# Where 576 token columns are divided between two matmuls, in four feed forwards

## The chip, the cores and the metric

The kernel runs on one core of one Trainium2 chip, in one launch. The metric is device time in microseconds. The engines are called PE (TensorE, matmuls), PEld (TensorE's weight loads, which overlap its matmuls), DVE (VectorE), ACT (ScalarE), POOL (GpSimd) and SP (SyncE, which issues most DMAs).

## What is computed

A step of a trunk of two layers of width 1024, for 512 prompt tokens and 8 sequences of 8 sample tokens, 576 tokens together. Each layer is a half feed forward, a mixer and another half feed forward, each behind an RMS norm that is shifted, scaled and gated by rows that are computed from a condition (adaLN). The mixer of layer 0 is a gated linear attention beside a spatial gate, that of layer 1 an mLSTM. What matters here is the feed forward, of hidden width 2816:

```python
def _swiglu(x, w_gate, w_up, w_down):
    return (jax.nn.silu(x @ w_gate) * (x @ w_up)) @ w_down

h = _modulate(_rms_norm(x, W['ffn_norm'][l, 0]), sh1, sc1)
x = x + 0.5 * g1[:, None, :] * _swiglu(h, W['ffn_w_gate'][l, 0], W['ffn_w_up'][l, 0], W['ffn_w_down'][l, 0])
```

It is computed four times: (layer 0, first), (0, second), (1, first), (1, second), called (0,0), (0,1), (1,0), (1,1) below.

## The kernel before, in words

Activations lie with features on the 128 partitions and tokens along the free axis: `x` is 8 tiles of 128 x 576. The first 512 columns are the prompt's, the last 64 the sample's. A product takes a 128 x 128 block of weights as the stationary operand and streams the tokens past it.

Precision is kept by splitting. A weight `w` and an activation `x` in float32 are each cut into a high and a low part of type float32r (`wh`, `wl`, `xh`, `xl`), and a product is `wh xh + wh xl + wl xh`. `w_split` (L183 on ACT, L184 on DVE) cuts the weights, which arrive by DMA in the order of use; `hilo` (L402, L403) cuts the activations.

`tile3` issues the three terms for one block of weights. A matmul writes at most 512 columns, a bank of PSUM, so the 576 token columns are divided: each term is two matmuls of 288 columns (`HT`) with the same weights, L203. `dense_gen` runs `tile3` over the row tiles of a product and hands the accumulator, `psd`, to whoever evacuates it; there are two such accumulators of two banks each. Before, each half of `psd` starts at the beginning of its bank, and readers see the two halves as a 3-D view (`v2`).

In `ffn` the hidden features come in three groups of 8, 7 and 7 tiles. For each tile the gate and the up product run over 8 row tiles; ACT takes the silu of the first (L470), DVE multiplies with the second (L477), and the result is cut into `hh` and `hl`. After a group the 8 output tiles run over the group's tiles (`psd<-hh` and `psd<-hl` in the profile), and `x_add` (L411, L413, L415) adds them to `x` on DVE, the prompt's columns with one gate and the sample's with one gate per sequence. So a feed forward has 22 x 2 x 8 row tiles for gate and up and 8 x 22 for down, three terms each. In layer 0 and before, `fill` puts matmuls of the adaLN rows (L256) between the products.

At the end of a feed forward `finish` sums the last squares over the features (`sumsq`, L319, L325), and the next `norm` follows from their sum. The mixers use the same `dense`, `pair_gen` and `x_add`; other matmuls are issued by their own lines, in float32 or float32r: L537 (float32r, 512 columns), L781 and L782 (float32r, 384 columns), L1399 and L256 (float32, 512 columns), L1498 and L1500 (one and four columns; the latter in float32r). A matmul in float32 stands in the profile as two rows.

The order on each engine is the order in which the program issues the instructions.

Of the kernel before, what the change touches and what calls it, by code (L numbers as in the profile page):

```python
# [25 lines left out]
PB = TP - HT  # L26
# [9 lines left out]
def _lhs(w):  # L36
    """[K, M] -> [128, (K/128) M]: row k*128+p, column m sits at [p, k*M+m]."""
    k, m = w.shape
    return w.reshape(k // P, P, m).transpose(1, 0, 2).reshape(P, -1)
# [22 lines left out]
def rows_units(key, c0):  # L62
    """Four units of two row tiles each, of 512 columns, for products that keep tokens on partitions."""
    for u in range(4):
        yield (1024, lambda a, u=u: _lhs(a[key][0][u * 256:(u + 1) * 256, c0:c0 + 512]))


def pair_units(key, m0, order):
    """Two column tiles of a square weight in turns of four row tiles."""
    for h in range(0, len(order), 4):  # L70
        yield (KD * P, lambda a, h=h: np.concatenate([_lhs(a[key][0][k * P:k * P + P, m * P:m * P + P]) for m in (m0, m0 + 1) for k in order[h:h + 4]], 1))
# [37 lines left out]
# parts of the constants that sit side by side, [128, ...] each  # L109
# [5 lines left out]
def cut(t, parts):  # L115
    """Views of a tile that holds such parts."""
    out, c0 = {}, 0
    for name, shape in parts.items():
        n = int(np.prod(shape))
        v = t[:, c0:c0 + n]  # L120
        if len(shape) > 1:
            ax = "abcd"[:len(shape)]
            v = v.rearrange(f"p ({' '.join(ax)}) -> p {' '.join(ax)}", **dict(zip(ax, shape)))
        out[name] = v
        c0 += n
    return out


class Trunk:
    def __init__(self, ctx, tc, ins, outs):  # L130
# [19 lines left out]
        # weight stream  # L150
# [7 lines left out]
        # ada stream  # L158
# [5 lines left out]
        self.queue = []  # L164

# [32 lines left out]
    def tile3(self, ps, wh, wl, xh, xl, start, stop):  # L198
        """ps[:, half, :HT] (+)= w^T x over one 128-row tile, w = wh + wl and x = xh + xl."""
        mm = self.nc.tensor.matmul  # L200
        for j, (w, xx) in enumerate(((wh, xh), (wh, xl), (wl, xh))):
            for a in range(2):
                mm(ps[:w.shape[1], a, :HT], w, xx[:, a * HT:(a + 1) * HT], start=start and j == 0, stop=stop and j == 2)  # L203

    def dense_gen(self, xs, order, evac):
        ps = self.psd.tile([P, 2, 512], F32, name="psd", tag="psd")
        n = len(order)
        for j in range(n):
            if j % 4 == 0:
                wh, wl = self.piece()  # L210
            c = slice(j % 4 * P, j % 4 * P + P)
            k = order[j]
            self.tile3(ps, wh[:, c], wl[:, c], xs[0][k], xs[1][k], j == 0, j == n - 1)
            if j < n - 1:
                yield
        evac(ps)
        yield
# [7 lines left out]
    def pair_gen(self, xs, order):  # L225
        """Two products whose weights come in turns of four row tiles."""
        ps = [self.psd.tile([P, 2, 512], F32, name="psd", tag="psd") for _ in range(2)]
        for j in range(len(order)):
            if j % 4 == 0:
                ws = [self.piece(), self.piece()]  # L230
            c = slice(j % 4 * P, j % 4 * P + P)
            for (wh, wl), p in zip(ws, ps):
                self.tile3(p, wh[:, c], wl[:, c], xs[0][order[j]], xs[1][order[j]], j == 0, j == len(order) - 1)
            yield ps if j + 1 == len(order) else []
# [41 lines left out]
    def mod_post(self, blk, m):  # L276
        """Keeps a shift, a norm's gain with its scale, or a gate (halved before the half sub-layers)."""
        nc = self.nc
        l, w = (2, blk - 18) if blk >= 18 else divmod(blk, 9)
        s = l * 3 + w // 3  # L280
        if w % 3 == 0:
            nc.vector.tensor_copy(self.sh[:, s], m)
        elif w % 3 == 1:
            nc.vector.scalar_tensor_tensor(out=self.am[:, s], in0=m, scalar=1.0,
                                           in1=self.gn[:, s, :].unsqueeze(2).to_broadcast([P, KD, NC]), op0=ALU.add, op1=ALU.mult)
        else:
            nc.vector.tensor_scalar(out=self.gm[:, s], in0=m, scalar1=1.0 if w == 5 else 0.5, scalar2=None, op0=ALU.mult)
# [7 lines left out]
    def fill_mm(self, n):  # L295
        """Up to n steps, none that evacuates a group."""
# [12 lines left out]
    def rsqrt(self, out, in_, scale, tmp):  # L309
        """out = (in_ * scale + EPS) ** -0.5"""  # L310
# [22 lines left out]
    def norm(self, s, ss, hook=None, mid=None):  # L333
        """xh + xl = rms_norm(x) * am + shift."""
# [45 lines left out]
    def final(self, s, ss):  # L380
        """The last norm, into the output."""
# [23 lines left out]
    def x_add(self, m, ps, g):  # L405
        """x[:, m] += g * ps, g by sequence."""
        nc = self.nc
        x = self.x[:, m, :]
        for a, n in ((0, HT), (1, PB)):
            xa = x[:, a * HT:a * HT + n]  # L410
            nc.vector.scalar_tensor_tensor(out=xa, in0=ps[:, a, :n], scalar=g[:, m, 0:1], in1=xa, op0=ALU.mult, op1=ALU.add)  # L411
        t = self.work.tile([P, TS], F32, name="xs", tag="xs")
        nc.vector.tensor_tensor(out=t.rearrange("p (b t) -> p b t", b=NS), in0=ps[:, 1, PB:HT].rearrange("p (b t) -> p b t", b=NS),  # L413
# [4 lines left out]
    def ada_pool(self, ctx, name, bufs, stop):  # L418
        """Room for adaLN weights that are loaded ahead, for the units before `stop`."""
# [4 lines left out]
    def first_norm(self, ss):  # L424
        """The norm that waits for its adaLN rows."""
# [13 lines left out]
    def ffn(self, l, i, ss, fills, gap):  # L439
# [7 lines left out]
        with ExitStack() as ctx:  # L447
# [6 lines left out]
            xs = self.xk()  # L454
            f0 = 0
            v2 = lambda t: t.rearrange("p (a n) -> p a n", a=2)
            for gi, n in enumerate(FGROUPS):
                hh = [hp.tile([P, T], F32R, name=f"hh{j}", tag=f"hh{j}") for j in range(n)]
                hl = [hp.tile([P, T], F32R, name=f"hl{j}", tag=f"hl{j}") for j in range(n)]
                for j in range(n):  # L460
# [9 lines left out]
                    nc.scalar.activation(v2(sg), pg[:, :, :HT], AF.Silu)  # L470
# [6 lines left out]
                    nc.vector.tensor_tensor(out=v2(h), in0=v2(sg), in1=pu[:, :, :HT], op=ALU.mult)  # L477
# [16 lines left out]
                f0 += n  # L494
            self.finish(ss)
# [5 lines left out]
    def finish(self, ss):  # L501
        """The last squares; adaLN matmuls fill TensorE until the next norm is through."""
# [25 lines left out]
    def rows_gen(self, evac):  # L528
        """x @ w for 512 columns with tokens on partitions."""
# [14 lines left out]
    def mixer0(self, ss):  # L544
        nc = self.nc
        tt, act = nc.vector.tensor_tensor, nc.scalar.activation
        v2 = lambda t: t.rearrange("p (a n) -> p a n", a=2)
        xs = self.xk()
        done = set()
        with ExitStack() as ctx:  # L550
# [13 lines left out]
            def ev_q(b, w):  # L564
                def evac(ps):
                    act(v2(qk[:, b, w]), ps[:, :, :HT], AF.Copy, scale=1.0 if w else 0.125)
# [14 lines left out]
            def ev_u(g):  # L581
                def evac(ps):
                    tt(out=v2(z[:, g]), in0=v2(z[:, g]), in1=ps[:, :, :HT], op=ALU.mult)
# [46 lines left out]
    def gla_gates(self, w2, ss, z, lh, ll, vr, vrs, sg):  # L630
        """The norm, the rows of log decays, and the spatial gate before its u."""
# [32 lines left out]
        for h in range(4):  # L664
            ps = self.dense(self.xk(), KS)
            act(sg[:, h].rearrange("p (a n) -> p a n", a=2), ps[:, :, :HT], AF.Silu)
# [57 lines left out]
    def gla_post(self, o, sg, gln, heads):  # L724
        """Norm over each head's values, gain and gate."""
# [34 lines left out]
    def gla(self, c, w2, lh, ll, vr, vrs, masks, bmask, qk, v, o, qm, ready, half):  # L760
# [10 lines left out]
        def expo(i, b):  # L771
            """exp of the summed log decays: from each block's middle, from the start and to the end of the rows."""
# [23 lines left out]
        def scores(i, b, hh, ke, qe):  # L796
            """S[s, t], level by level of the blocks that part s from t."""
# [124 lines left out]
    def operands(self, ctx, name):  # L922
        """Room for the parts of the normed rows."""
# [55 lines left out]
    def ml_in(self, w1):  # L979
        """The input projection, the convolution, and the rows that the gates give."""  # L980
# [4 lines left out]
        v2 = lambda t: t.rearrange("p (a n) -> p a n", a=2)  # L985
# [25 lines left out]
        def xm_block(f, ps):  # L1011
            xm = w1.tile([P, T], F32, name="xm", tag="xm", bufs=4)
            xms[f] = xm
            act(v2(xm), ps[:, :, :HT], AF.Copy)
# [46 lines left out]
        for f in range(MB):  # L1061
# [4 lines left out]
            act(v2(zs), ps[:, :, :HT], AF.Silu)  # L1066
# [14 lines left out]
    def ml_rows(self, w, pg):  # L1081
        """Per token and head: a = log input gate - F, F the summed log forget gates, M the running maximum of a, m = F + M."""
# [3 lines left out]
        v2 = lambda t: t.rearrange("p (a n) -> p a n", a=2)  # L1086
# [158 lines left out]
    def ml_sample(self, h):  # L1245
        """The sample's queries, keys and values, its scores and denominators."""
# [61 lines left out]
    def stack(self, h, j):  # L1308
        """Three copies of the sample's rows, for keys with their weights."""
# [6 lines left out]
    def ml_den(self, pd, em):  # L1316
        """max(den ** 2, exp(-m) ** 2)"""
# [7 lines left out]
    def ml_head(self, h):  # L1325
# [6 lines left out]
        # the prompt's projections  # L1332
        i4 = lambda t: t.rearrange("p (i c) -> p i c", c=P)

        def keys(j):
            """Keys with tokens on partitions, and their weights."""
# [28 lines left out]
        # its scores  # L1365
# [22 lines left out]
        # denominators and numerators  # L1388
# [23 lines left out]
    def ml_norm(self, pn, d2):  # L1412
        """The rows over their denominators, normed: (pn - mean) * (var + EPS * d2) ** -0.5."""
# [13 lines left out]
    def z_load(self, h, t):  # L1427
        """The gate with its gain and with skip and input, for a tile of tokens."""
# [4 lines left out]
    def ml_post(self, hn, t, z):  # L1433
        """Back to features on partitions, with gain, skip and gate, in two parts."""
# [18 lines left out]
    def ml_units(self, h, den):  # L1453
        """The sample's matrices: what they add to the outputs, and their update."""
# [29 lines left out]
    def ml_state(self, h):  # L1484
        """The prompt's matrix, and both groups' normalisers."""
# [44 lines left out]
def levels(n, chunk, sizes):  # L1530
    """0/1 patterns (the first over 16) of which rows s the decays of row t sum over, and of the pairs that a level holds."""
# [51 lines left out]
def pack(a):  # L1583
    """The inputs as the program takes them: cut, transposed and put side by side."""
# [72 lines left out]
```

## Time and profile before

| what | value |
|---|---|
| median of 2 runs | 2811.63 us (2810.9 to 2812.36) |
| span of the profiled execution, first to last instruction | 2806.7 us |
| TensorE busy | 2731.7 us, 97%, 19182 matmuls |
| VectorE busy | 1281.7 us, 46% |
| ScalarE busy | 839.5 us, 30% |
| mean granted TensorE clock | 0.983 |
| feed forward (0,0), from its first to its last product | 36.7 to 480.7 us |
| (0,1) | 822.1 to 1267.6 us |
| (1,0) | 1278.6 to 1704.6 us |
| (1,1) | 2363.5 to 2789.3 us |

The profiled execution is known by its span; the times of the runs lie some 5 us above it, which is what lies around the first and the last instruction. The busy time of a group of instructions is the time in which at least one of them is under way. The length of a single matmul's row (some 296 ns) holds its way through the array, in which the next one has already started; what a matmul costs in a stream is the time from its start to the next one's start, read from rows of the timeline.

### The profile page before, as it was taken

The page shows a single profiled execution, that of the slowest core. Times are in us where ns is not written, and L with a number is a line of the kernel's source. Part 1 is how long each engine was busy: PE and PEld are TensorE (multiplying, and loading weights), DVE is VectorE, ACT ScalarE, POOL GpSimd, SP SyncE. Part 2 cuts the span into 40 slices and gives each one's busy share as a digit, 9 for nine tenths or more (in the row PEclk, how much of TensorE's full clock was granted, in tenths as well). Part 3 has the DMA queues.
Part 4 walks back from the last instruction along what each step waited for, and adds up shares of the span by engine and source line. Part 5 has one row for each costly group of instructions (what it writes and reads, how often), then busy time and mean ns, then how long its engine had stood idle before and what let it go on. Part 6 is the DMA issues. An engine that isn't in the chain of part 4 may idle for free.

```text
span 2806.7 us, 45768 instructions
## 1 busy us (share of the span) xinstructions
PE 2731.7 (97%) x19182; PEld 2462.0 (88%) x19182; DVE 1281.7 (46%) x2578; ACT 839.5 (30%) x1508; POOL 193.4 (7%) x263
## 2 busy tenths in 40 slices
PE   6999999999999999999999999999999999999997
PEld 4899998787788999998999997998567667999997
DVE  4233334346562333345333337654776676333334
ACT  4222223432242222234222234334323324222223
POOL 1000000022110000001000004300110111000000
PEclk8999999999799999999999999999999999999999
DMA  7533224221146332223222244467885665222222
GB/s 288 214 122 136 83 82 138 67 77 45 56 166 255 136 136 83 84 83 113 83 83 77 85 143 164 151 177 240 304 295 213 235 244 195 89 83 82 84 76 73
DMA packets 114741, 388.49 MB, mean 138 GB/s; under 512 B 19416, under 2 KB 37096, under 8 KB 95720
## 3 DMA queue, kind: packets, MB, share of 16 engines
q1 hardware_dynamic: 102088, 336.62, 35.0%
q0 software_dynamic: 4880, 35.06, 3.2%
q10 hardware_dynamic: 7568, 13.90, 1.3%
q8 instruction: 151, 2.47, 0.3%
q14 instruction: 54, 0.44, 0.0%
HBM read 324.95 MB, written 60.59 MB: 137 GB/s over the span
## 4 chain that ended last, share of the span: by engine, by line
PE 90%; DVE 4%; ACT 2%; issue 1%; DMA 1%; POOL 1%; DVEq 0%; SPq 0%; ACTq 0%; POOLq 0%
PE psd L203 74%; PE psc L1494 2%; PE psd L537 2%; PE psa L256 1%; PE psc L1382 1%; PE psa L1465 1%; PE psc L1399 1%; PE psc L805 1%; DVE yn L363 1%; DMA adaw<-ada 1%; POOL qe L788 1%; DVE xl L353 1%; PE psd L1473 1%; PE psc L1348 1%; PE psd L1351 0%
## 5 line engine op out<-in xcount | busy, mean ns | idle before, releaser
L203 PE MATMUL psd<-xh,whi 128*128 128x288 f32 x3648 | 794.7, 299 | 11.5 <-ACT xh L364 7.7
L203 PE MATMUL psd<-xl,whi 128*128 128x288 f32 x3648 | 786.8, 297 | 7.2 <-DVE xl L353 6.8
L203 PE MATMUL psd<-xh,wlo 128*128 128x288 f32 x3648 | 784.3, 297 | 1.5 <-DVE wlo L184 1.5
L184 DVE TENSOR_TENSOR wlo<-wraw,whi 128x512 fp32r<-128x512 f32 (+1 forms) x696 | 459.2, 698 | 454.0 <-ACT whi L183 449.6
L203 PEld LDWEIGHTS psd<-xh,whi 128*128 128x128 f32 x3648 | 589.5, 190 | 55.1 <-issue 18.0
L203 PEld LDWEIGHTS psd<-xl,whi 128*128 128x128 f32 x3648 | 590.2, 190 | 12.5 <-DVE xl L353 11.9
L203 PEld LDWEIGHTS psd<-xh,wlo 128*128 128x128 f32 x3648 | 590.9, 190 | 1.8 <-DVE wlo L184 1.8
L183 ACT CAST whi<-wraw 128x512 fp32r<-128x512 f32 (+1 forms) x696 | 400.4, 609 | 411.0 <-PE psd L203 371.5
L203 PE MATMUL psd<-hh,whi 128*128 128x288 f32 x1408 | 301.4, 296 | 0.0
L203 PE MATMUL psd<-hh,wlo 128*128 128x288 f32 x1408 | 301.3, 295 | 0.0
L203 PE MATMUL psd<-hl,whi 128*128 128x288 f32 x1408 | 300.9, 295 | 0.0
L411 DVE SCALAR_TENSOR_TENSOR x<-psd,gm,x 128x288 f32<-128x288 f32 (+1 forms) x272 | 119.2, 480 | 345.3 <-PE psd L203 345.3
L203 PEld LDWEIGHTS psd<-hh,whi 128*128 128x128 f32 x1408 | 226.7, 188 | 1.7 <-issue 1.7
L203 PEld LDWEIGHTS psd<-hl,whi 128*128 128x128 f32 x1408 | 226.6, 188 | 0.0
L203 PEld LDWEIGHTS psd<-hh,wlo 128*128 128x128 f32 x1408 | 226.4, 188 | 0.0
L477 DVE TENSOR_TENSOR h<-sg,psd 128x576 f32<-128x576 f32 x88 | 66.4, 754 | 349.2 <-PE psd L203 349.2
L402 ACT CAST hh<-h 128x576 fp32r<-128x576 f32 x88 | 59.3, 674 | 488.7 <-DVE h L477 488.7
L470 ACT ACTIVATE sg<-psd 128x576 f32<-128x576 f32 x88 | 57.4, 653 | 359.8 <-PE psd L203 359.8
L349 POOL TENSOR_TENSOR yn<-x,rstd 128x576 f32<-128x576 f32 x30 | 49.3, 1651 | 1067.3 <-ACT rstd L377 1010.1
L403 DVE TENSOR_TENSOR hl<-h,hh 128x576 fp32r<-128x576 f32 x88 | 66.8, 759 | 65.2 <-ACT hh L402 65.2
L203 PE MATMUL psd<-hz,whi 128*128 128x288 f32 x512 | 95.5, 309 | 0.9 <-DVE kc L1286 0.9
L1477 DVE SCALAR_TENSOR_TENSOR cu<-cu,wd,psd 128x512 f32<-128x512 f32 x128 | 87.0, 742 | 15.2 <-PE psd L1473 14.5
(331 smaller groups left out, 2251.6 us busy)
## 6 DMA issues: line engine op xcount, KB each, us to landing
wraw<-wall SPq DMA_DIRECT2D x284, 512.0 KB, 3.6
adaw<-ada SPq DMA_DIRECT2D x80, 1024.0 KB, 7.5
cu<-mC SPq DMA_DIRECT2D x32, 1024.0 KB, 5.7
Cs<-cu POOLq DMA_DIRECT2D x32, 1024.0 KB, 6.1
wraw<-wall SPq DMA_DIRECT2D x64, 448.0 KB, 3.2
szp<-zp SPq DMA_DIRECT2D x32, 256.0 KB, 2.6
bx<-sx SPq DMA_DIRECT2D x16, 512.0 KB, 6.0
zt<-szp SPq DMA_DIRECT2D x16, 512.0 KB, 7.7
```

What stands on the lines that cost most here:

```text
L183: nc.scalar.copy(hi[:, :n], raw)
L184: nc.vector.tensor_tensor(out=lo[:, :n], in0=raw, in1=hi[:, :n].bitcast(F32), op=ALU.subtract)
L203: mm(ps[:w.shape[1], a, :HT], w, xx[:, a * HT:(a + 1) * HT], start=start and j == 0, stop=stop and j == 2)
L349: eng.tensor_tensor(out=y, in0=self.x[:, k, :], in1=rstd, op=ALU.mult)
L402: self.nc.scalar.copy(hi, y)
L403: self.nc.vector.tensor_tensor(out=lo, in0=y, in1=hi.bitcast(F32), op=ALU.subtract)
L411: nc.vector.scalar_tensor_tensor(out=xa, in0=ps[:, a, :n], scalar=g[:, m, 0:1], in1=xa, op0=ALU.mult, op1=ALU.add)
L470: nc.scalar.activation(v2(sg), pg[:, :, :HT], AF.Silu)
L477: nc.vector.tensor_tensor(out=v2(h), in0=v2(sg), in1=pu[:, :, :HT], op=ALU.mult)
L537: mm(ps[i], xx[:, k, self.tokens(i)], w, start=k == 0 and j == 0, stop=k == KD - 1 and j == 2)
L1477: nc.vector.scalar_tensor_tensor(out=cu[:, g], in0=cu[:, g], scalar=dec, in1=pu[:, i], op0=ALU.mult, op1=ALU.add)
L1494: mm(pc, self.v[:, s, g * P:(g + 1) * P], self.wk[:, s], start=s == 0, stop=s == 3)
```

## The change

`tile3` gets a column `c = self.cut`. The first matmul of a pair takes the tokens 0 to `c` and writes them at the end of the first bank, columns 512 − c to 512; the second takes the tokens `c` to 576 and writes from the beginning of the second bank. So the 576 columns lie side by side in `psd`, and `cols` gives them as one 2-D view, which all evacuations now read. `x_add` takes the prompt's 512 columns in one operation instead of two of 288 and 224 columns. `cut` is 288 (`HT`) outside the feed forwards; in them it is 288 in (0,0), 320 in (0,1), 384 in (1,0) and 512 in (1,1), so that the pairs are 288+288, 320+256, 384+192 and 512+64.

```diff
@@ __init__
+        self.cut = HT
@@ tile3
         mm = self.nc.tensor.matmul
+        c = self.cut
+        parts = [(slice(512 - c, 512), slice(0, c)), (slice(512, 512 + T - c), slice(c, T))]
         for j, (w, xx) in enumerate(((wh, xh), (wh, xl), (wl, xh))):
-            for a in range(2):
-                mm(ps[:w.shape[1], a, :HT], w, xx[:, a * HT:(a + 1) * HT], start=start and j == 0, stop=stop and j == 2)
+            for o, t in parts:
+                mm(ps[:w.shape[1], o], w, xx[:, t], start=start and j == 0, stop=stop and j == 2)
+
+    def psum(self):
+        return self.psd.tile([P, 1024], F32, name="psd", tag="psd")
+
+    def cols(self, ps):
+        return ps[:, 512 - self.cut:512 - self.cut + T]
@@ dense_gen
-        ps = self.psd.tile([P, 2, 512], F32, name="psd", tag="psd")
+        ps = self.psum()
...
-        evac(ps)
+        evac(self.cols(ps))
@@ x_add
-        for a, n in ((0, HT), (1, PB)):
-            xa = x[:, a * HT:a * HT + n]
-            nc.vector.scalar_tensor_tensor(out=xa, in0=ps[:, a, :n], scalar=g[:, m, 0:1], in1=xa, op0=ALU.mult, op1=ALU.add)
+        xp = x[:, :TP]
+        nc.vector.scalar_tensor_tensor(out=xp, in0=ps[:, :TP], scalar=g[:, m, 0:1], in1=xp, op0=ALU.mult, op1=ALU.add)
...
@@ ffn
             xs = self.xk()
+            self.cut = {(0, 0): 288, (0, 1): 320, (1, 0): 384, (1, 1): 512}[l, i]
...
-                    nc.scalar.activation(v2(sg), pg[:, :, :HT], AF.Silu)
+                    nc.scalar.activation(sg, pg, AF.Silu)
...
-                    nc.vector.tensor_tensor(out=v2(h), in0=v2(sg), in1=pu[:, :, :HT], op=ALU.mult)
+                    nc.vector.tensor_tensor(out=h, in0=sg, in1=pu, op=ALU.mult)
...
+            self.cut = HT
             self.finish(ss)
```

On TensorE, in the last group of down products of (1,1), this stood there before (`hh` and `hl` are the high and low parts of the hidden tiles, `whi` and `wlo` those of the weights; the number after hh or hl names one tile, and x2 joins rows that are alike):

```order
L203 MATMUL psd<-hh_25326,whi 128x288 x2
L203 MATMUL psd<-hl_25333,whi 128x288 x2
L203 MATMUL psd<-hh_25326,wlo 128x288 x2
L203 MATMUL psd<-hh_25327,whi 128x288 x2
L203 MATMUL psd<-hl_25334,whi 128x288 x2
```

And now at the same place:

```order
L205 MATMUL psd<-hh_25198,whi 128x512
L205 MATMUL psd<-hh_25198,whi 128x64
L205 MATMUL psd<-hl_25205,whi 128x512
L205 MATMUL psd<-hl_25205,whi 128x64
L205 MATMUL psd<-hh_25198,wlo 128x512
L205 MATMUL psd<-hh_25198,wlo 128x64
L205 MATMUL psd<-hh_25199,whi 128x512
L205 MATMUL psd<-hh_25199,whi 128x64
```

The order of the products and the number of matmuls are the same; a wide and a narrow one alternate.

On VectorE, in the x_adds of the same place, before:

```order
L184 TENSOR_TENSOR wlo<-wraw,whi 128x512
L184 TENSOR_TENSOR wlo<-wraw,whi 128x384
L321 TENSOR_TENSOR sqa<-sqa,sq 128x576
L411 SCALAR_TENSOR_TENSOR x<-psd,gm,x 128x288
L411 SCALAR_TENSOR_TENSOR x<-psd,gm,x 128x224
L413 TENSOR_TENSOR xs<-psd,gm 128x64
L415 TENSOR_TENSOR x<-x,xs 128x64
```

And now:

```order
L184 TENSOR_TENSOR wlo<-wraw,whi 128x512
L184 TENSOR_TENSOR wlo<-wraw,whi 128x384
L330 TENSOR_TENSOR sqa<-sqa,sq 128x576
L419 SCALAR_TENSOR_TENSOR x<-psd,gm,x 128x512
L421 TENSOR_TENSOR xs<-psd,gm 128x64
L423 TENSOR_TENSOR x<-x,xs 128x64
```

One operation stands where there were two, in the same place; nothing else on VectorE moved, and the other engines have the same instructions in the same order.

More of the change, by code (lines that the diff above doesn't have):

```diff
@@ L25 @@
 KS = list(range(8))
-PB = TP - HT
 NC = 1 + NS
@@ L225, in pair_gen @@
     def pair_gen(self, xs, order):
-        ps = [self.psd.tile([P, 2, 512], F32, name="psd", tag="psd") for _ in range(2)]
+        ps = [self.psum() for _ in range(2)]
         for j in range(len(order)):
@@ L233, in pair_gen @@
                 self.tile3(p, wh[:, c], wl[:, c], xs[0][order[j]], xs[1][order[j]], j == 0, j == len(order) - 1)
-            yield ps if j + 1 == len(order) else []
+            yield [self.cols(p) for p in ps] if j + 1 == len(order) else []
     def dense_pair(self, xs, order):
@@ L408, in x_add @@
         x = self.x[:, m, :]
-        for a, n in ((0, HT), (1, PB)):
-            xa = x[:, a * HT:a * HT + n]
-            nc.vector.scalar_tensor_tensor(out=xa, in0=ps[:, a, :n], scalar=g[:, m, 0:1], in1=xa, op0=ALU.mult, op1=ALU.add)
+        xp = x[:, :TP]
+        nc.vector.scalar_tensor_tensor(out=xp, in0=ps[:, :TP], scalar=g[:, m, 0:1], in1=xp, op0=ALU.mult, op1=ALU.add)
         t = self.work.tile([P, TS], F32, name="xs", tag="xs")
-        nc.vector.tensor_tensor(out=t.rearrange("p (b t) -> p b t", b=NS), in0=ps[:, 1, PB:HT].rearrange("p (b t) -> p b t", b=NS),
+        nc.vector.tensor_tensor(out=t.rearrange("p (b t) -> p b t", b=NS), in0=ps[:, TP:].rearrange("p (b t) -> p b t", b=NS),
                                 in1=g[:, m, 1:].unsqueeze(2).to_broadcast([P, NS, LS]), op=ALU.mult)
@@ L454, in ffn @@
             xs = self.xk()
+            self.cut = {(0, 0): 288, (0, 1): 320, (1, 0): 384, (1, 1): 512}[l, i]
             f0 = 0
-            v2 = lambda t: t.rearrange("p (a n) -> p a n", a=2)
             for gi, n in enumerate(FGROUPS):
@@ L546, in mixer0 @@
         tt, act = nc.vector.tensor_tensor, nc.scalar.activation
-        v2 = lambda t: t.rearrange("p (a n) -> p a n", a=2)
         xs = self.xk()
@@ L565, in evac @@
                 def evac(ps):
-                    act(v2(qk[:, b, w]), ps[:, :, :HT], AF.Copy, scale=1.0 if w else 0.125)
+                    act(qk[:, b, w], ps, AF.Copy, scale=1.0 if w else 0.125)
                     done.add((b, w))
@@ L582, in evac @@
                 def evac(ps):
-                    tt(out=v2(z[:, g]), in0=v2(z[:, g]), in1=ps[:, :, :HT], op=ALU.mult)
+                    tt(out=z[:, g], in0=z[:, g], in1=ps, op=ALU.mult)
                 return evac
@@ L665, in gla_gates @@
             ps = self.dense(self.xk(), KS)
-            act(sg[:, h].rearrange("p (a n) -> p a n", a=2), ps[:, :, :HT], AF.Silu)
+            act(sg[:, h], ps, AF.Silu)
         self.log_exp()
@@ L984, in ml_in @@
         gp = nc.gpsimd
-        v2 = lambda t: t.rearrange("p (a n) -> p a n", a=2)
         sm = lambda t: t.rearrange("p (b t) -> p b t", b=NS)
@@ L1013, in xm_block @@
             xms[f] = xm
-            act(v2(xm), ps[:, :, :HT], AF.Copy)
+            act(xm, ps, AF.Copy)
             nc.scalar.dma_start(self.sx[f, :, 0], xm[:, :TP])
@@ L1065, in ml_in @@
             zs = w1.tile([P, T], F32, name="zs", tag="cy", bufs=2)
-            act(v2(zs), ps[:, :, :HT], AF.Silu)
+            act(zs, ps, AF.Silu)
             zp = w1.tile([P, 2, T], F32, name="zp", tag="zp", bufs=2)
@@ L1085, in ml_rows @@
         ts, cp = nc.vector.tensor_scalar, nc.vector.tensor_copy
-        v2 = lambda t: t.rearrange("p (a n) -> p a n", a=2)
         sm = lambda t: t.rearrange("p (b t) -> p b t", b=NS)
```

## The prediction

> **What bounds the kernel now.** I read the page first, for the engine that carries the time; then the stages by windows; then single rows of matmuls and weight loads, for the price of each width.
>
> ```profile
> span 2806.7 us, 45768 instructions
> PE 2731.7 (97%) x19182; PEld 2462.0 (88%) x19182; DVE 1281.7 (46%) x2578; ACT 839.5 (30%) x1508; POOL 193.4 (7%) x263
> PE psd L203 74%; PE psc L1494 2%; PE psd L537 2%; PE psa L256 1%; PE psc L1382 1%; PE psa L1465 1%; PE psc L1399 1%; PE psc L805 1%; DVE yn L363 1%; DMA adaw<-ada 1%; POOL qe L788 1%; DVE xl L353 1%; PE psd L1473 1%; PE psc L1348 1%; PE psd L1351 0%
> L203 PE MATMUL psd<-hh,whi 128*128 128x288 f32 x1408 | 301.4, 296 | 0.0
> L203 PE MATMUL psd<-hl,whi 128*128 128x288 f32 x1408 | 300.9, 295 | 0.0
> ```
>
> The chain that ended last is TensorE for the most part, and L203, the line that the change edits, alone holds 74% of it. Before the matmuls of the down products TensorE never idles (0.0). There are as many weight loads (PEld) as matmuls: each matmul has a load of its own, also the second one of a pair that uses the same weights.
>
> The stages follow, in order of time the feed forwards (0,0), (0,1), (1,0), (1,1), and last 100 us from the middle of (1,0). The columns are the stretch, its length, busy time and instructions of TensorE, its loads, VectorE, ScalarE and GpSimd, then the granted clock and the DMA.
>
> ```profile
> 36.70:480.70 444.00, 442.82 (x3305) 425.74 (x3306) 162.45 (x313) 119.77 (x203) 4.25 (x3) 0.99 0.37 130
> 822.10:1267.60 445.50, 444.76 (x3309) 428.08 (x3310) 162.49 (x318) 118.62 (x201) 4.27 (x3) 1.00 0.37 128
> 1278.60:1704.60 426.00, 424.28 (x3173) 423.11 (x3174) 159.75 (x304) 118.71 (x201) 5.00 (x4) 1.00 0.30 100
> 2363.50:2789.30 425.80, 424.18 (x3173) 423.01 (x3174) 158.75 (x302) 117.64 (x199) 4.29 (x3) 1.00 0.25 77
> 1300.00:1400.00 100.00, 100.00 (x752) 100.00 (x751) 32.94 (x54) 26.29 (x46) 0.00 (x0) 1.00 0.27 85
> ```
>
> TensorE is busy without a break at a granted clock of 1.00, while VectorE works 160 of 426 us, ScalarE 119, and the DMA engines under 0.4. So whatever the change adds to TensorE in these stages is added to the time; the others only gain slack. In the steady stretch 752 matmuls took 100 us: 133 ns from start to start for 288 columns, 266 ns for a pair. By the code one feed forward has 22·2·8·3 pairs for gate and up and 8·22·3 for down, 1,584 pairs; 1,584 · 266 ns = 421 us of the 426.
>
> **The change part by part.** The number and order of matmuls stay; the widths of a pair change. What I need is the spacing of 512, 384, 320 and 256 columns, and then of 192 and 64, all with 128 columns of weights in f32r.
>
> For 512 columns the mixer's L537 has such matmuls, for 384 the pair L781 and L782 (timeline rows: start, length, what):
>
> ```profile
> 573.94 1.08 PE L537 MATMUL psd<-whi,xh 128*128 128x512 f32 x4
> 574.86 0.40 PE L537 MATMUL psc<-whi,xh 128*64 128x512 f32 x1
> 575.10 1.08 PE L537 MATMUL psd<-whi,xl 128*128 128x512 f32 x4
> 576.01 0.40 PE L537 MATMUL psc<-whi,xl 128*64 128x512 f32 x1
> 576.25 1.08 PE L537 MATMUL psd<-wlo,xh 128*128 128x512 f32 x4
> ...
> 614.26 0.33 PE L781 MATMUL psc<-vr,lh 128*128 128x384 f32 x1
> ...
> 615.15 0.33 PE L782 MATMUL psc<-vr,ll 128*128 128x384 f32 x1
> 615.32 0.42 PE L203 MATMUL psd<-xh,whi 128*128 128x288 f32 x2
> ```
>
> From 573.94 to 576.25 start ten matmuls: 231 ns each. From 614.26 to 615.32 start six: 177 ns each. With 133 ns at 288 the three lie on a line of 0.44 to 0.46 ns a column and some 4 ns fixed. On it 320 columns cost 148 ns, 256 cost 118, 192 cost about 90, 64 cost 30 to 35.
>
> A narrow matmul leaves less time to load the next weights. What a load costs, the trace shows twice. The rows of L537 have loads of 128 and of 64 columns (min/median/max ns); and in L1498 and L1500 the moving operand has 1 and 4 columns, so that the loads alone remain, those of L1500 in f32r:
>
> ```profile
> L537 PEld LDWEIGHTS psd<-whi,xh x64: 186/188/192, 492.2 to 582.1; 128*128 128x128 f32 x64
> L537 PEld LDWEIGHTS psc<-whi,xh x16: 133/134/135, 493.1 to 582.3; 128*64 128x64 f32 x16
> ...
> 2011.23 0.36 PE L1500 MATMUL psc<-selr,kc 128*128 128x4 f32 x2
> 2011.45 0.36 PE L1498 MATMUL psc<-ones,t 128*128 128x1 f32 x2
> ...
> 2012.57 0.36 PE L1500 MATMUL psc<-selr,kc 128*128 128x4 f32 x2
> ```
>
> 64 more columns of weights take 54 ns more, so 128 take 108 ns of pure loading; the rest of the 188 is latency that runs beside other work. From 2011.23 to 2012.57 start twelve matmuls with next to nothing to stream: 112 ns each. I take 112 ns as the least spacing of two loads. It does not bind 288 columns (133) nor 256 (118), and it binds 192 and 64.
>
> The sum, pair by pair:
> - (0,0), 288+288: the same widths at another place in PSUM: 0.
> - (0,1), 320+256: 148 + 118 = 266 against 266: 0. The 256 clear the load by 6 ns only; with 2 ns a pair either way this is 3 us.
> - (1,0), 384+192: 177 + 112 = 289, 23 ns more; 1,584 times: +36.4 us.
> - (1,1), 512+64: 231 + 112 = 343, 77 ns more; 1,584 times: +122.0 us.
>
> The Trainium skill, "TensorE: Matmul & The Clock Gate", section "Back-to-back issue gap", states a sustained spacing of about 81 ns with the load for 128 columns and 131 ns for 512. The trace differs on both: 112 ns with 4 columns and 231 ns with 512. By its 81 ns, an estimate of mine, only the 64 columns would be bound, and the sum would be some 73 us.
>
> In `x_add` two operations on 288 and 224 columns become one on 512. On the way to the next norm the last of them ends late; so it is at the end of (0,1):
>
> ```profile
> 1267.68 0.88 DVE x L411 x2
> 1268.56 0.14 DVE xs L413
> ...
> 1268.72 0.23 DVE x L415
> ...
> L1477 DVE SCALAR_TENSOR_TENSOR cu<-cu,wd,psd 128x512 f32<-128x512 f32 x128 | 87.0, 742 | 15.2 <-PE psd L1473 14.5
> ```
>
> The two took 0.88 us; one of the same kind on 512 columns from PSUM took 0.74. That is 0.14 us at the end of each of six sub-layers: −0.8 us. The other x_adds lie under TensorE's matmuls, as do the evacuations whose two runs of 288 become one run of 576 across two banks: the same elements, 0. Should these get slower, the 266 us in which VectorE idles in such a stage cover it.
>
> The sum is 36.4 + 122.0 − 0.8 = +157.6 us. On the profiled span of 2806.7 us that makes 2964.3. The median, 2811.6, lies 4.9 us above the span; I carry this over: **2969 us**.
>
> What the trace doesn't show is a matmul of 64 to 255 columns in f32r behind a wide one. From below its price is the streaming line (90 and 35 ns, no change at all). The row nearest to it is the load-bound one, at 112. Around that value I take 98 to 133: 133 is the spacing that these very operands have, if something besides the load is in it; below 108 the load itself would have to go faster than its rows. 133 adds 21 ns · 3,168 narrow matmuls = 67 us (3036); 98 takes off 44 us (2925).
>
> **The rivals.**
>
> *The load doesn't bind, and the time doesn't change.* The narrow matmul uses the weights of the wide one, and the load ran ahead in its 231 ns. If the repeated load were dropped, or two could be kept ahead, the pair would cost what streams: 231 + 35 = 266 and 177 + 90 = 267, so 2811. This decides at a spacing of 70 ns: (70 − 35) · 1,584 = 55 us, under 2%. For it speaks that steady loads are fully hidden today. Against it: the rows have a load for every matmul, and twelve short ones in a row kept 112 ns though all could have been loaded ahead. The same section of the skill gives an isolated gap of about 60 cycles at up to 64 columns, which would make this rival true; no load is counted in that. Chance 8%, and 3% for a spacing between 70 and 98 ns (about 2870 to 2925), where the 81 ns would lie.
>
> *Narrow f32r falls to the pace of plain f32.* Plain f32 runs slower per column:
>
> ```profile
> 2309.64 2.31 PE L1399 MATMUL psc<-v,pt 128*128 128x512 f32 x5
> 2311.79 0.38 PE L1439 MATMUL psc<-ident,sq 128*128 128x128 f32 x2
> ...
> L256 PE MATMUL psa<-adaw,cs 128*32 128x512 f32 x640 | 81.3, 615 | 4.7 <-DMA adaw<-ada 4.7
> ```
>
> Five started in 2.15 us, 430 ns for 512 columns, and a plain f32 matmul is two such rows (L256 is called 320 times and has 640). That is 1.68 ns a column: 322 ns for 192 columns; 64 stay at the load. (1,0) would cost (177 + 322 − 266) · 1,584 = 369 us, (1,1) the 122: 3302 us. Nothing in the rows asks for it (1 and 4 columns cost the same), but no row of 64 to 255 columns excludes it. Chance 6%.
>
> *The load waits until the narrow matmul has streamed.* Then a pair costs wide + narrow + 108: 177 + 90 + 108 = 375 and 231 + 35 + 108 = 374, together 217 ns · 1,584 = 344 us: 3155. Against it: loads run fully beside 288 columns in the steady window, both busy for all of its 100 us. Chance 4%.
>
> *That it gets faster* would need 12 ns off each of the 4,752 changed pairs for 2%; the fixed part of a spacing is 4 to 7 ns, so no mechanism here reaches it. 2% for what I don't see.
>
> **How the numbers follow.** The load-bound case has 77% and gives 2969. 2% of the time, 56 us, is about what a measurement tells from no change. Slower by over 2% are the load-bound case, the spacing of 70 to 98, the plain-f32 pace and the serial load: 77 + 3 + 6 + 4 = 90%. Within 2% is the unbound load, 8%; faster 2%. The range 2925 to 3036 is the likeliest case with its own bounds, which is nearly 8 in 10.
>
> **What would show it.** In the window of (1,0) the stage should last about 462 us, in that of (1,1) 548, in (0,0) and (0,1) 444 and 446 as now. In a steady 100 us of (1,1) there should be about 583 matmuls instead of 752, in (1,0) about 692, and starts alternating 231 and 112 ns. The load row should stay near 188 ns and the clock at 1.00; a lower clock with the array streaming 70% of a pair would add to the sum. I am wrong if (1,1) keeps its 426 us (the load is hidden), if (1,0) grows by more than (1,1) (a narrow matmul's own pace), or if both grow by the same some 170 us (a serial load).

## The result, and the profile after

The changed kernel takes 2959.78 us (median, 2959.08 to 2960.49) against 2811.63 us before: 1.0528 times as long, with a 95% interval of 1.0511 to 1.0545. The forecast was 2969 us in a range of 2925 to 3036.

The page of the changed kernel (L205 is the line that was L203, L419 the x_add's operation on 512 columns):

```profile
span 2957.3 us, 45632 instructions
PE 2884.3 (98%) x19182; PEld 2546.7 (86%) x19182; DVE 1264.5 (43%) x2442; ACT 839.3 (28%) x1508; POOL 193.5 (7%) x263
L205 PE MATMUL psd<-hh,whi 128*128 128x288 f32 (+6 forms) x1408 | 318.4, 307 | 0.0
L205 PE MATMUL psd<-hl,whi 128*128 128x288 f32 (+6 forms) x1408 | 318.3, 307 | 0.0
L419 DVE SCALAR_TENSOR_TENSOR x<-psd,gm,x 128x512 f32<-128x512 f32 x136 | 102.1, 751 | 407.3 <-PE psd L205 407.3
```

There are as many matmuls and loads as before, and TensorE still never idles ahead of the down products. The rows of its loads cover a smaller share of the time (86% after 88%): the loads no longer follow each other evenly, as the rows below show.

The windows of (0,0), (0,1), (1,0) and (1,1), and 100 us from the middle of the last two (length, then busy time and instructions of TensorE, its loads, VectorE, ScalarE and GpSimd, then clock and DMA):

```profile
37.30:481.40 444.10, 441.70 (x3305) 424.13 (x3306) 159.52 (x290) 119.76 (x203) 4.31 (x3) 0.99 0.38 129
823.20:1269.10 445.90, 444.26 (x3309) 427.07 (x3310) 159.56 (x295) 118.52 (x201) 4.28 (x3) 1.00 0.38 128
1279.90:1733.60 453.70, 453.35 (x3173) 452.88 (x3174) 156.91 (x281) 118.82 (x201) 5.00 (x4) 1.00 0.30 94
2392.20:2940.00 547.80, 547.53 (x3173) 478.55 (x3174) 155.79 (x279) 117.40 (x199) 4.24 (x3) 0.99 0.20 60
1350.00:1450.00 100.00, 100.00 (x705) 100.00 (x704) 33.23 (x62) 21.91 (x37) 0.00 (x0) 1.00 0.26 75
2600.00:2700.00 100.00, 100.00 (x587) 87.45 (x585) 24.06 (x36) 20.36 (x36) 0.00 (x0) 1.00 0.21 63
```

Against 444.0, 445.5, 426.0 and 425.8 us before, the stages grew by 0.1, 0.4, 27.7 and 122.0 us. That is 150.2 of the 150.6 us by which the span grew (2957.3 − 2806.7); the rest of the kernel is untouched.

The granted clock is what it was but for the start of (1,1), where it stood at half for some 10 us. The rows are the first 11.5 us of the stage before, then the first 11.8 us and the rest of it in the changed kernel:

```profile
2363.50:2375.00 11.50, 9.88 (x65) 8.71 (x66) 11.18 (x20) 8.77 (x13) 4.29 (x3) 1.00 0.13 45
...
2392.20:2404.00 11.80, 11.53 (x39) 9.67 (x40) 11.41 (x20) 9.09 (x14) 4.24 (x3) 0.57 0.13 43
2404.00:2940.00 536.00, 536.00 (x3137) 468.88 (x3136) 144.38 (x259) 108.31 (x186) 0.00 (x0) 1.00 0.20 60
```

This spell costs some 4 us: with pairs of the same widths and a granted clock of 1.00 the stage lasts 543.7 us in two of the experiments below (512+64 in all four; the narrow matmul first). So some 118 of the 122.0 us belong to the widths. Why the clock fell there in this execution is not shown.

Where the time sits inside a pair is seen in the starts of the weight loads. Single rows of the timeline, four loads from (1,1) and three from (1,0); in each group the first load is that of a wide matmul, the second that of the narrow one with the same weights, and so on:

```profile
2800.22 0.19 PEld L205 LDWEIGHTS psd<-xh,whi 128*128 128x128 f32 x1
2800.33 0.19 PEld L205 LDWEIGHTS psd<-xh,whi 128*128 128x128 f32 x1
2800.56 0.19 PEld L205 LDWEIGHTS psd<-xl,whi 128*128 128x128 f32 x1
2800.67 0.19 PEld L205 LDWEIGHTS psd<-xl,whi 128*128 128x128 f32 x1
...
1600.28 0.19 PEld L205 LDWEIGHTS psd<-xh,whi 128*128 128x128 f32 x1
1600.39 0.19 PEld L205 LDWEIGHTS psd<-xh,whi 128*128 128x128 f32 x1
1600.57 0.19 PEld L205 LDWEIGHTS psd<-xl,whi 128*128 128x128 f32 x1
```

I read them so: a load starts when the matmul before it begins to stream. Then the wide matmul's load, at 2800.22, runs while the 64 columns stream; 0.11 us later the wide matmul begins and the narrow one's load with it; 0.23 us later the wide one is through. In (1,0) the spacings are 0.11 and 0.18. The narrow matmul has the same 0.11 us at 192 and at 64 columns.

### The profile page after: what moved, and what is told of

It reads as the page before. It is cut to its first block, busy times and chain, and to the rows that moved or that the text cites. A ratio compares the mean times of both kernels' runs of the same rounds, so it can differ in the third digit from the quotient of the medians.

```text
span 2957.3 us, 45632 instructions
## 1 busy us (share of the span) xinstructions
PE 2884.3 (98%) x19182; PEld 2546.7 (86%) x19182; DVE 1264.5 (43%) x2442; ACT 839.3 (28%) x1508; POOL 193.5 (7%) x263
## 4 chain that ended last, share of the span: by engine, by line
PE 91%; DVE 4%; ACT 1%; issue 1%; POOL 1%; DMA 1%; DVEq 0%; SPq 0%; ACTq 0%; POOLq 0%
PE psd L205 75%; PE psc L1500 2%; PE psd L546 2%; PE psa L265 1%; PE psc L1388 1%; PE psa L1471 1%; PE psc L1405 1%; PE psc L813 1%; DVE yn L372 1%; DMA adaw<-ada 1%; POOL qe L796 1%; PE psd L1479 1%; PE psc L1354 1%; PE psd L1357 0%; DVE xl L362 0%
## 5 line engine op out<-in xcount | busy, mean ns | idle before, releaser
L205 PE MATMUL psd<-xh,whi 128*128 128x288 f32 (+3 forms) x3648 | 830.1, 309 | 11.7 <-ACT xh L373 7.6
L205 PE MATMUL psd<-xl,whi 128*128 128x288 f32 (+3 forms) x3648 | 822.2, 307 | 6.6 <-DVE xl L362 6.2
L205 PE MATMUL psd<-xh,wlo 128*128 128x288 f32 (+3 forms) x3648 | 820.3, 306 | 1.5 <-DVE wlo L184 1.5
L205 PEld LDWEIGHTS psd<-xh,whi 128*128 128x128 f32 x3648 | 569.2, 190 | 72.1 <-issue 18.1
L205 PEld LDWEIGHTS psd<-xl,whi 128*128 128x128 f32 x3648 | 570.0, 190 | 26.0 <-DVE xl L362 10.6
L205 PEld LDWEIGHTS psd<-xh,wlo 128*128 128x128 f32 x3648 | 570.6, 191 | 16.6 <-DVE wlo L184 1.8
L205 PE MATMUL psd<-hh,wlo 128*128 128x288 f32 (+6 forms) x1408 | 318.8, 307 | 0.0
L205 PE MATMUL psd<-hh,whi 128*128 128x288 f32 (+6 forms) x1408 | 318.4, 307 | 0.0
L205 PE MATMUL psd<-hl,whi 128*128 128x288 f32 (+6 forms) x1408 | 318.3, 307 | 0.0
L419 DVE SCALAR_TENSOR_TENSOR x<-psd,gm,x 128x512 f32<-128x512 f32 x136 | 102.1, 751 | 407.3 <-PE psd L205 407.3
L205 PEld LDWEIGHTS psd<-hh,whi 128*128 128x128 f32 x1408 | 216.0, 189 | 9.8 <-issue 1.7
L205 PEld LDWEIGHTS psd<-hh,wlo 128*128 128x128 f32 x1408 | 216.0, 189 | 7.3
L205 PEld LDWEIGHTS psd<-hl,whi 128*128 128x128 f32 x1408 | 216.1, 189 | 7.2
L205 PE MATMUL psd<-hz,whi 128*128 128x288 f32 x512 | 94.6, 306 | 0.2 <-DVE kc L1292 0.2
```

Of the source, the lines that this page charges most:

```text
L205: mm(ps[:w.shape[1], o], w, xx[:, t], start=start and j == 0, stop=stop and j == 2)
L419: nc.vector.scalar_tensor_tensor(out=xp, in0=ps[:, :TP], scalar=g[:, m, 0:1], in1=xp, op0=ALU.mult, op1=ALU.add)
```

## The experiments

The theory after the result is that of the forecast: behind a narrow matmul the load of the next weights is exposed, about 110 ns less what the narrow one streams. The rivals: a least time of its own for narrow matmuls, whatever they load (A); the narrow matmul's own load being the one exposed (B); a fixed extra below 256 columns; and a part played by the layout of the accumulators or by x_add.

**Half the weight columns for the wide matmuls of (1,1).** Half of these products' outputs for the prompt's tokens is left out.

```diff
-            for o, t in parts:
-                mm(ps[:w.shape[1], o], w, xx[:, t], start=start and j == 0, stop=stop and j == 2)
+            for a, (o, t) in enumerate(parts):
+                n = 64 if c == 512 and a == 0 and not (start and j == 0) and not (stop and j == 2) else 128
+                mm(ps[:n, o], w[:, :n], xx[:, t], start=start and j == 0, stop=stop and j == 2)
```

> As the changed kernel, but in (1,1) the 512-column matmuls use only the first 64 of the 128 weight columns (except the first and the last that write a product), so half of these products' outputs is left out. The load that a 64-column matmul has to cover is then of 64 weight columns, some 55 to 58 ns. Theory (the load of the next wide matmul is exposed behind the narrow one): pair 231+57 = 288 instead of 342, 1,448 pairs, 78 us less than the changed kernel: 2882 us. Rival A (a narrow matmul has a least time of its own of some 110 ns): 2960 us. Rival B (what is exposed is the narrow matmul's own load): 2960 us.

Measured: 2885.5 us, 1.0256 times the time before (1.0241 to 1.0271). The window of (1,1), and its loads:

```profile
2394.00:2867.60 473.60, 473.33 (x3173) 399.34 (x3174) 155.66 (x279) 117.37 (x199) 4.26 (x3) 1.00 0.23 70
...
2700.00 0.14 PEld L206 LDWEIGHTS psd<-hl,whi 128*64 128x64 f32 x1
2700.06 0.19 PEld L206 LDWEIGHTS psd<-hl,whi 128*128 128x128 f32 x1
2700.30 0.13 PEld L206 LDWEIGHTS psd<-hh,wlo 128*64 128x64 f32 x1
```

The load of 64 weight columns is followed by the next one after 0.06 us instead of 0.11, though the narrow matmul that streams meanwhile has its 64 token columns as before. The stage is 74 us shorter than in the changed kernel's profile, and 70 us shorter than the 543.7 us at full clock, where the theory had 78. Rivals A and B had no change.

**Half the weight columns for the narrow matmuls of (1,1).** Half of the outputs for the sample's tokens is left out; the edit is the same but for one place.

```diff
-                n = 64 if c == 512 and a == 0 and not (start and j == 0) and not (stop and j == 2) else 128
+                n = 64 if c == 512 and a == 1 and not (start and j == 0) and not (stop and j == 2) else 128
```

> The counterpart: in (1,1) the 64-column matmuls use only the first 64 of the 128 weight columns (except the first and the last that write a product), so half of the outputs for the sample tokens is left out; the wide ones keep 128. Theory (the exposed load is the next wide one's, the narrow one's is hidden under 231 ns): no change against the changed kernel, 2960 us. Rival A (least time of a narrow matmul): 2960 us. Rival B (the narrow matmul's own load is exposed): 2882 us.

Measured: 2960.81 us, 1.0528 times (1.0511 to 1.0546), like the changed kernel.

```profile
2385.00:2933.50 548.50, 548.24 (x3173) 399.09 (x3174) 155.68 (x279) 117.39 (x199) 4.26 (x3) 1.00 0.19 60
...
2700.03 0.19 PEld L206 LDWEIGHTS psd<-xl,whi 128*128 128x128 f32 x1
2700.14 0.14 PEld L206 LDWEIGHTS psd<-xl,whi 128*64 128x64 f32 x1
2700.38 0.19 PEld L206 LDWEIGHTS psd<-xh,wlo 128*128 128x128 f32 x1
```

The narrow matmul's load became shorter (0.14 after 0.19 us) and the spacings stayed where they were to 0.01 us: 0.11 behind the start of the wide one's load, 0.24 behind that of its own. The theory forecast this, and with the run before it decides against A and B: what counts is the size of the load that follows a narrow matmul.

**The narrow 64 columns divided into 32 and 32 in (1,1).**

```diff
+        if c == 512:
+            parts = [(slice(0, 512), slice(0, 512)), (slice(512, 544), slice(512, 544)), (slice(544, 576), slice(544, 576))]
...
-                mm(ps[:w.shape[1], o], w, xx[:, t], start=start and j == 0, stop=stop and j == 2)
+                mm(ps[:w.shape[1], o], w, xx[:, t], start=start and j == 0 and t.start != 544, stop=stop and j == 2 and t.stop != 544)
```

> As the changed kernel, with the 64 columns of a pair in (1,1) divided once more, into 32 and 32, so that 1,584 narrow matmuls and their loads come on top. Theory (every narrow matmul has a load behind it, of 109 ns): 1,584 times 109 ns = 173 us more than the changed kernel, 3133 us. Rival (loads can run two ahead under the 512 columns, and a narrow matmul costs its issue alone, some 28 ns from start to start): 2960 + 44 = 3004 us or less.

Measured: 3132.26 us, 1.1135 times (1.1115 to 1.1155).

```profile
2395.80:3114.90 719.10, 718.89 (x4757) 651.99 (x4758) 155.68 (x280) 117.46 (x199) 4.26 (x3) 1.00 0.14 46
...
2700.22 0.19 PEld L207 LDWEIGHTS psd<-xh,whi 128*128 128x128 f32 x1
2700.33 0.19 PEld L207 LDWEIGHTS psd<-xl,whi 128*128 128x128 f32 x1
2700.44 0.19 PEld L207 LDWEIGHTS psd<-xl,whi 128*128 128x128 f32 x1
2700.68 0.19 PEld L207 LDWEIGHTS psd<-xl,whi 128*128 128x128 f32 x1
```

1,584 more narrow matmuls cost 171.3 us against the changed kernel's profile (719.1 − 547.8), 108 ns each, or 111 ns each against the 543.7 us at full clock, without a column more to stream. The rows are the load of the second 32 columns of one term and then all three loads of the next, 0.11, 0.11 and 0.24 us apart: no second load ran ahead under the wide matmul. The first 0.11 lies between two matmuls that write the same bank of PSUM, so a change of bank is not what costs the time.

**Other widths.** 304+272 in (0,0), 336+240 in (0,1), 352+224 in (1,0), 448+128 in (1,1).

```diff
-            self.cut = {(0, 0): 288, (0, 1): 320, (1, 0): 384, (1, 1): 512}[l, i]
+            self.cut = {(0, 0): 304, (0, 1): 336, (1, 0): 352, (1, 1): 448}[l, i]
```

> Other places of division: 304+272 in (0,0), 336+240 in (0,1), 352+224 in (1,0), 448+128 in (1,1). Theory (pair = wide's stream + the larger of narrow's stream and a load of about 110 ns): 140+125 = 265, 154+111 = 265, 161+110 = 271, 203+110 = 313 against 266 before: about 0, 0, +8 and +75 us, in all 2894 us. Rival (a narrow matmul under 256 columns pays a fixed extra of some 20 ns, whatever the load): (0,1) and (1,0) about +32 us each, in all some 2950 us.

Measured: 2891.73 us, 1.028 times (1.0259 to 1.03). The four stages:

```profile
37.10:482.20 445.10, 444.04 (x3305) 426.88 (x3306) 159.40 (x290) 119.61 (x203) 4.27 (x3) 0.99 0.37 129
824.10:1268.40 444.30, 442.64 (x3309) 425.49 (x3310) 159.54 (x295) 118.64 (x201) 4.29 (x3) 1.00 0.38 129
1279.20:1715.60 436.40, 434.82 (x3173) 433.70 (x3174) 156.89 (x281) 118.61 (x201) 5.00 (x4) 1.00 0.30 98
2375.50:2874.50 499.00, 498.74 (x3173) 476.15 (x3174) 155.66 (x279) 117.30 (x199) 4.27 (x3) 1.00 0.21 66
```

Against before: +1.1, −1.2, +10.4 and +73.2 us, where the theory had about 0, 0, 8 and 75. A narrow matmul of 240 columns costs nothing extra and one of 224 little (10.4 us are 6.6 ns a pair), so there is no fixed extra of some 20 ns below 256. By these two stages the knee, where the narrow one's own stream gets as short as the load, lies between 240 and 224 columns.

**512+64 in all four feed forwards.**

```diff
-            self.cut = {(0, 0): 288, (0, 1): 320, (1, 0): 384, (1, 1): 512}[l, i]
+            self.cut = 512
```

> 512+64 in all four feed forwards. Theory (exposed load, the same in every stage): 122 us more in each, 2811.6 + 488 = 3300 us. Rival (the adaLN matmuls between the products of (0,0) and (0,1), or the weight stream there, take up part of it): less, by what those two stages hide.

Measured: 3281.63 us, 1.1666 times (1.1645 to 1.1687).

```profile
37.20:604.30 567.10, 566.94 (x3305) 482.00 (x3306) 159.28 (x290) 119.61 (x203) 4.23 (x3) 0.99 0.30 103
943.30:1505.60 562.30, 561.88 (x3309) 477.97 (x3310) 159.50 (x295) 118.53 (x201) 4.27 (x3) 1.00 0.30 103
1516.40:2061.10 544.70, 544.43 (x3173) 475.96 (x3174) 156.85 (x281) 118.59 (x201) 4.99 (x5) 1.00 0.24 78
2715.90:3259.60 543.70, 543.28 (x3173) 474.75 (x3174) 155.69 (x279) 117.37 (x199) 4.27 (x3) 1.00 0.20 61
```

The stages grew by 123.1, 116.8, 118.7 and 117.9 us. Neither the adaLN matmuls of (0,0) and (0,1) nor the weight stream hides any of it. The median is 18 us short of the 3300. Of this, 11.5 us lie in the stages, which grew by 476.5 us and not by 488: a load is exposed for 108 to 109 ns, where I had put in 112. Some 6 us lie outside of them (the span grew by 470.1 us only) and are not explained.

**The narrow matmul first in (1,1).**

```diff
-            for o, t in parts:
+            for o, t in parts[::-1] if c == 512 else parts:
```

> As the changed kernel, with the 64-column matmul of each pair issued before the 512-column one in (1,1). Theory (one load has 64 columns to hide under, wherever it stands): 2960 us; the load exposed is now that of the wide matmul of the same weights. Rival (the cost comes from the bank of PSUM that is switched, or from new weights behind a narrow matmul; here the load behind the narrow one is of the same weights): less than 2960, down to 2838.

Measured: 2965.33 us, 1.0542 times (1.0522 to 1.0561). (1,0), which this leaves alone, and (1,1):

```profile
1281.20:1743.50 462.30, 461.90 (x3173) 461.44 (x3174) 156.88 (x282) 118.61 (x201) 5.02 (x5) 1.00 0.29 92
2402.90:2946.60 543.70, 543.52 (x3173) 474.74 (x3174) 155.57 (x279) 117.35 (x199) 4.28 (x3) 1.00 0.20 61
```

(1,1) is 4 us shorter than in the changed kernel's profile, not 122, and the 4 us are those of the half clock, which this execution doesn't have in (1,1). Three loads of (1,1), of a wide matmul behind the narrow one with the same weights, then of the narrow and the wide one of the next term:

```profile
2700.09 0.19 PEld L205 LDWEIGHTS psd<-xh,whi 128*128 128x128 f32 x1
2700.20 0.19 PEld L205 LDWEIGHTS psd<-xl,whi 128*128 128x128 f32 x1
2700.43 0.19 PEld L205 LDWEIGHTS psd<-xl,whi 128*128 128x128 f32 x1
```

The first load is of the very weights that the narrow matmul is using, and it is waited for all the same, 0.11 us. Of the rival's two parts this excludes the new weights; the bank changes in either order, and the division into 32 and 32 has excluded that.

But (1,0), with the same instructions as in the changed kernel, took 462.3 us instead of 453.7. I ran both programs again for this.

> The changed kernel once more, for the stage (1,0): it took 453.7 us in the changed kernel's profile and 462.3 us in the profile with the narrow matmul first in (1,1), though the two have the same instructions up to the end of (1,0). If the pace of 384-column streams belongs to the execution, the stage may come out at either; if it belongs to the program, at 453.7.

> The kernel with the narrow matmul first in (1,1) once more, for the stage (1,0). If the pace belongs to the program: 462.3 us again; if to the execution: either 453.7 or 462.3. The load theory expects 2960 to 2966 us in all.

Measured: 2950.74 us for the changed kernel (1.0497 times, 1.0467 to 1.0528) and 2952.84 us with the narrow one first (1.0505, 1.0474 to 1.0535). In these profiles 100 us of (1,0) held, in this order:

```profile
1500.00:1600.00 100.00, 100.00 (x705) 100.00 (x704) 33.14 (x64) 22.72 (x40) 0.00 (x0) 1.00 0.26 77
...
1500.00:1600.00 100.00, 100.00 (x705) 100.00 (x704) 32.70 (x63) 22.71 (x40) 0.00 (x0) 1.00 0.25 79
```

Both are at 705 matmuls, where the odd execution had 692:

```profile
1500.00:1600.00 100.00, 100.00 (x692) 100.00 (x691) 33.47 (x64) 22.53 (x40) 0.00 (x0) 1.00 0.24 74
```

These two were taken on another chip than the odd one. But the three versions with half the weight columns or with 32 and 32, taken on the same chip as the odd one, have the same instructions in (1,0) too, and there the stage lasted 453.9, 453.7 and 453.7 us. So the program alone doesn't set the pace: of seven profiles of this stage one is slower. Its load is the same, 108 ns by the median of the starts in the trace; what differs is the spacing in which the 384 columns stream, 182 ns instead of 176. What sets this stays open; both timed executions of the odd version were long (2965.68 and 2964.99 us), so it need not change from one execution to the next. On the whole time the stage's 8.6 us weigh 0.3%, and when run side by side the two orders take the same time.

**288+288 in all four, in the new layout.**

```diff
-            self.cut = {(0, 0): 288, (0, 1): 320, (1, 0): 384, (1, 1): 512}[l, i]
+            self.cut = HT
```

> The new layout of the accumulators and the single x_add of 512 columns, with 288+288 in all four feed forwards. Theory (the weight load under a narrow matmul is the whole cost): 2811 us, the time before less some 0.8 us of x_add, every feed forward as before (426 us in (1,0) and (1,1)). Rival (layout or x_add carry a part of the 148 us, or hide a gain that offset it): off by more than 5 us from 2811.

> The kernel with 288+288 everywhere once more, for the small difference: the first comparison had a ratio of 0.9979 with an interval of 0.9968 to 0.999. Theory (0.8 us from x_add): a ratio of 0.9997, 1 within the interval. Rival (the new layout gives some 5 us): again a ratio near 0.998 with an interval below 1.

Measured: 2808.05 us, 0.9979 times the time before (0.9968 to 0.999), and again 2808.34 us, 0.9984 times (0.9975 to 0.9994). The windows of (1,0) and (1,1):

```profile
1278.40:1704.40 426.00, 425.28 (x3173) 424.65 (x3174) 156.80 (x281) 118.61 (x201) 4.98 (x4) 1.00 0.32 100
2362.90:2788.90 426.00, 424.33 (x3173) 423.16 (x3174) 155.72 (x279) 117.46 (x199) 4.28 (x3) 1.00 0.25 77
```

With the widths undone the whole slowdown is gone, so it is all of the widths. Both times the interval lies below 1: the ratios are 0.16 and 0.21% lower, some 5 us, where I had 0.8 from x_add and expected 1 within the interval; here the rival came true. (1,0) and (1,1) don't show it (426.0 us twice), so where the rest comes from is open. This is the one version that is faster than both kernels, by that little.

## Why the prediction was right

- *"Whatever the change adds to TensorE in these stages is added to the time."* The four stages hold 150.2 of the span's 150.6 us.
- *(0,0) and (0,1): 0.* Measured 0.1 and 0.4 us. The 256 columns do cover the load, and the sweep's 240 still do.
- *(1,1): 231 + 112 = 343 ns, +122.0 us.* The stage grew by 122.0 us in this execution; in the four stages of the kernel with 512+64 everywhere by 116.8 to 123.1. The agreement to a tenth is chance: at a clock of 1.00 the stage grew by some 118 us, since the load is exposed for 108 to 109 ns rather than 112, and in this execution the half clock at the stage's start put 4 us back.
- *(1,0): 177 + 112 = 289 ns, +36.4 us.* Measured +27.7. Both terms were a little large, the load's above all: the 100 us hold 705 matmuls, a pair of 284 ns, and the starts of the loads in the trace are 108 and 176 ns apart (medians). The 112 came from rows of one and four columns, the 177 from six matmuls of the mixer; why twelve matmuls without a stream are 112 ns apart and not 108 is not shown. At the odd execution's pace (692 matmuls, a pair of 289 ns) the stage took 462.3 us, the forecast's 462, but by chance: the loads took their 108 ns there too, and only the wide streams were longer.
- *x_add: −0.8 us.* The operation took 751 ns on the page, for 0.88 us of two before, 0.13 us less where 0.14 was forecast. In the span it can't be seen: what lies outside the four stages grew by 0.4 us. The gain of layout and x_add together, some 5 us with 288+288 everywhere, is larger and not explained.
- *The median 4.9 us above the span.* This is not, as said ahead of the prediction, all time around the first and the last instruction: where both are known, a timed run lies 1.8 us above its own span (2959.08 against 2957.3), so the profiled execution before was a faster one than those timed. After the change the median lies 2.5 us above the span. Of the 9 us by which the forecast was high, 2.4 come from this and most of the rest from (1,0).
- *The rival in which the load doesn't bind* needed a spacing under 70 ns. With half the weight columns in the wide matmuls' loads the spacing did fall to 0.06 us, and then the time came down with it, to 2885.5; a whole load behind a narrow matmul was hidden in no run, not even when the same weights were loaded twice in a row. The Trainium skill, "TensorE: Matmul & The Clock Gate", section "LDWEIGHTS (loading the stationary operand)", gives a load's time in ns as its number of weight columns over 1.2, whatever the rows; by an estimate from it that is 107 and 53 ns for 128 and 64 columns. The trace's spacings of 0.11 and 0.06 us agree.
- *Plain f32's pace* would have made (1,0) grow by 369 us, *the serial load* both stages by some 170: neither has anything in the rows, where 192 and 64 columns have the same 0.11 us.

## What to carry to other kernels

A matmul must stream long enough to cover the load of the weights that come next, also where they are the same weights again; here 128 columns of them took 108 to 109 ns, which some 230 token columns cover. A division of the columns costs nothing as long as both parts stay above that, as 336+240 did; a wide part and a remainder pay one load less the remainder's stream, per pair. Price such a thing from the starts of the loads in the trace, not from the lengths of the matmuls' rows.

## What the runs showed that I had not expected

A matmul's row can start before its stream, as I read these rows. In (1,1) the wide matmul's row begins 0.03 us behind the start of its own load, while the load has most of its 0.11 us still to go (rows of the timeline of the changed kernel; x2 joins a wide matmul and the narrow one after it):

```profile
2800.22 0.30 PEld L205 LDWEIGHTS psd<-xh,whi 128*128 128x128 f32 x2
2800.25 0.50 PE L205 MATMUL psd<-xh,whi 128*128 128x512 f32 x2
```

From one such pair to the next are 0.34 us. Read by the starts of the matmuls' rows alone, the wide one would seem to take 0.31 us and the narrow one 0.03, and the narrow one's load would look like the one that is waited for; yet 512 columns took 231 ns in the mixer. Only the starts of the loads, and the two runs with half the weight columns, tell it the right way.

The other surprise is that the same instructions kept another pace through a whole stage in one of seven profiles, 289 instead of 284 ns a pair in (1,0), at a granted clock of 1.00 in both.
